# Sample products in groups of four, a partition move by DMA, a last block product ended tile by tile, and eight products on GpSimd, in a streaming encoder step

## The chip, the cores and the metric

The kernel runs on one core of a Trainium2 chip. The core has a matmul engine (PE in the profile, its weight loads PEld), VectorE (DVE), ScalarE (ACT), GpSimd (POOL) and SyncE (SP), which in this kernel issues nearly all transfers. Each engine works off its own list of instructions in order; instructions of different engines meet only at semaphores. Matmuls read from the on-chip memory SBUF and write to PSUM, eight banks of 128 x 512 float32. The metric is the device time of one execution in microseconds (us), the median of several runs.

## The reference, cut to what matters

One layer of a hybrid encoder is applied to 1024 prompt frames and to 32 frames of a running stream (the sample). The change lies in the last product of the layer, the down projection of the feed-forward part, and in the norm and residual behind it:

```
def conv_ffn(xn, buf, w_up, conv_w, conv_b, w_down):
    up = xn @ w_up
    up, buf = causal_dwconv(up, buf, conv_w, conv_b)
    gate, val = jnp.split(up, 2, axis=-1)
    return (jax.nn.gelu(gate, approximate=True) * val) @ w_down, buf
...
    h, ffn_buf = conv_ffn(rms_norm(x, g_ffn_pre[l]), ...)
    x = x + rms_norm(h, g_ffn_post[l])
```

`w_down` is 2816 x 1024, and everything is float32.

## The kernel before, in words

**What runs ahead.** Projections, the three kinds of token mixer, an output projection and the up projection fill the first 1143 us. The up projection leaves the activated rows as 22 tiles `h` of 128 features x (1024 prompt columns and 32 sample columns, with gaps) in DRAM (`h_d`). While it runs, sums of quarters of `w_down` that are needed later are formed in DRAM (`ws_d`).

**Down projection (`down_all`, L1464).** Prompt rows (two halves of 512), features (two halves of 11 tiles, NP = 11) and output columns (two halves of 512) make 2 x 2 blocks on each side, and seven block products P1 to P7 on sums and differences of quarters replace eight. They run in the order P2, P1, P4, P6, P5, P7, P3. `run` (L1480 on) does one of them: for each feature tile p of 0 to 10 it fetches the operands and issues four times three matmuls, one triple for each 128-row tile i, into four PSUM banks. The triple (`mm3`, L100 to L103) is a float32 product from two rounded halves: high by high, high by low, low by high. The halves come from `halves_of` and `split`: ACT casts the high half (L107) and DVE subtracts it from the source (L110). In the profile the line of a matmul is that of `mm3`; the tile names `q` and `x` tell the bank, and `P2w`, `P2h` the operands.

**Raw weights.** `down_raw` (L1419, and L1424 for the summed quarters) loads 512 KB pieces through SP into a ring of two pools with two buffers each. A piece of P1 or P2 holds both column halves, since the sample needs both; the block product uses the left half alone, though `down_operands` splits both. The halves of the activations go through four buffers ("hop"), those of the weights through seven ("op").

**The sample.** Its 32 rows are multiplied with the unsplit weights in float32 while P2 and P1 hold them. `sample_products` (L1461) is called at odd p and at the last p, for both p of the pair and both column halves j: four products, each onto its own 32 partitions of one bank (`s1` in P2, `s2` in P1), so that partitions 0 to 31 hold column half 0 of even p, 32 to 63 half 1 of even p, 64 to 95 half 0 of odd p and 96 to 127 half 1 of odd p. `keep` is the sum of both banks (copy L1545, add L1554). Two float32 matmuls with a selection matrix `sel` (L1558) add the even and odd parts and bring both halves to partitions 0 to 31. The bank of `s2` is one of the three "big" ones that P4 uses next.

**The end.** `norm_of` (L1512 on) squares a 128 x 512 half row tile on ACT with a running sum (L1514) and multiplies it by the gain on DVE (L1515). `close` (L1517 on) turns the sums into a scale by three small operations on POOL (L1518, L220, L221) and, for each column half, multiplies, adds the residual on DVE (L1522) and stores through SP (L1523). The lower four row tiles live in `CA`, the upper four in `CB`. `CB` is complete before P3 begins; upper tiles are normed and closed while P3's first four feature tiles run. `run("P3", ..., 4)` leaves out the last four feature tiles, and the loop behind it issues them row tile by row tile, with the add to `CA` (L1615), the norm and the close of each tile behind it.

**What sets the order.** The program is written in the order above, but each engine's list is laid out by a scheduler that simulates the program and may put a later instruction ahead of an earlier one when its operands are ready sooner. `tc.issue_after(ins)` makes what is issued inside it, on the engine of `ins`, stand behind `ins`. `behind["SP"]` and `behind["POOL"]` are such marks that the kernel keeps already.

Of the kernel before, what the change touches and what calls it, by code (L numbers as in the profile page):

```python
# [8 lines left out]
F32 = mybir.dt.float32  # L9
# [3 lines left out]
AF = mybir.ActivationFunctionType  # L13
ALU = mybir.AluOpType
# [5 lines left out]
DEC = 32  # L20
# [11 lines left out]
GAP_S, SMP, GAP_P = 512, 514, 546  # L32
# [59 lines left out]
def body(ctx: ExitStack, tc: tile.TileContext, a: dict):  # L92
    nc = tc.nc
    act, dve, pool, pe, sp = nc.scalar, nc.vector, nc.gpsimd, nc.tensor, nc.sync
# [5 lines left out]
    def mm3(ps, lh, rh, first, last, **kw):  # L100
        pe.matmul(ps, lh[0], rh[0], start=first, stop=False, **kw)  # L101
        pe.matmul(ps, lh[0], rh[1], start=False, stop=False, **kw)  # L102
        return pe.matmul(ps, lh[1], rh[0], start=False, stop=last, **kw)  # L103

    def split(hi, lo, src, eng=None, heng=None):
        if heng is None:
            act.copy(hi, src)  # L107
        else:
            heng.tensor_copy(hi, src)
        (eng or pool).tensor_tensor(lo, src, hi.bitcast(F32), op=ALU.subtract)  # L110
# [7 lines left out]
    psb = ctx.enter_context(tc.tile_pool(name="psb", bufs=3, space=PSUM))  # L118
# [68 lines left out]
    ident = const("ident", [128, 128])  # L187
# [30 lines left out]
    def rstd_of(out, ss, n, cols, width, eps=EPS):  # L218

        pool.tensor_scalar(out, ss, 1.0 / width, eps, op0=ALU.mult, op1=ALU.add)  # L220
        pool.tensor_tensor(out, out, mhalf[:n, :cols], op=ALU.pow)  # L221
# [996 lines left out]
    behind = {}  # L1218
# [168 lines left out]
    NP = NF // 2  # L1387
# [20 lines left out]
    wraws = {}  # L1408
# [18 lines left out]
    hts = {}  # L1427
# [12 lines left out]
    def halves_of(src, name, pool_, tag, bufs):  # L1440
        t = pool_.tile([128, 2, 512], F32R, tag=tag, name=name, bufs=bufs)
        split(t[:, 0], t[:, 1], src, dve)
        return t[:, 0], t[:, 1]

    def down_operands(ph, kind, p, early=False):
        down_raw(kind, p)
        h = halves_of(ablk(*ASRC[kind], p), f"{kind}h{p}", ph, "hop", 4)
        wp = (ph, "hop", 4) if early else (praw[1], "op", 7)
        if kind in ("P1", "P2"):
            r = wraws[kind, p]  # L1450
            w = [halves_of(r[:, j], f"{kind}w{p}{j}", *wp) for j in range(2)]
        else:
            w = [halves_of(wraws[kind, p // 2][:, p % 2], f"{kind}w{p}", *wp)]
        return h, w

    def sample_products(ps, k, p):

        for q in range(p - p % 2, p + 1):
            for j in range(2):
                r = 64 * (q % 2) + DEC * j  # L1460
                pe.matmul(ps[r:r + DEC], hts[q + NP * k][:, SMP:SMP + DEC], wraws["P2" if k else "P1", q][:, j],  # L1461
                          start=q < 2, stop=q >= NP - 2)

    def down_all(ph, pc, begun, late):  # L1464

        CA = pc.tile([128, 4, 2, 512], F32, name="ca")
        CB = pc.tile([128, 4, 2, 512], F32, name="cb")
        gp = pc.tile([128, 1024], F32, name="gp")
        sp.dma_start(gp, a["grows"][1:2, :].broadcast_to([128, 1024]))
        sel = pc.tile([128, 2 * DEC], F32, name="sel")  # L1470
        dve.tensor_tensor(sel, ident[:, 0:2 * DEC], ident[:, 2 * DEC:], op=ALU.add)
# [5 lines left out]
        def w_banks(name):  # L1477
            return [psf.tile([128, 512], F32, tag="sx", name=f"{name}0", bufs=1)] + \
                [psb.tile([128, 512], F32, tag="big", name=f"{name}{i}", bufs=3) for i in range(1, 4)]

        def run(kind, banks, first, last, each=None, n_end=0):
            end = []
            for p in range(NP):
                ops = begun.pop((kind, p), None) or down_operands(ph, kind, p)
                if p >= NP - n_end:
                    end.append((p, ops))
                    continue
                h, w = ops
                wi = w[0]
                for i in range(4):  # L1490
                    c = slice(128 * i, 128 * i + 128)
                    mm3(banks[i], (h[0][:, c], h[1][:, c]), wi, first and p == 0, last and p == NP - 1, skip_group_check=True)
                if each:
                    each(p, w)
            return end
# [11 lines left out]
        def fourth_sum(p):  # L1507
            f0, f1 = hts[p], hts[p + NP]
            dve.scalar_tensor_tensor(f1[:, :512], f1[:, :512], -1.0, f0[:, :512], op0=ALU.mult, op1=ALU.subtract)

        def norm_of(u, n, src, half, ss):
            c = slice(512 * half, 512 * half + 512)  # L1512
            jk = pc.tile([128, 512], BF16, tag="fjk", name=f"gjk{u}{half}", bufs=2)
            act.activation(jk[:n], src, AF.Square, accum_out=ss[:n, 2 + half:3 + half])  # L1514
            dve.tensor_tensor(src, src, gp[:n, c], op=ALU.mult)  # L1515

        def close(u, n, y, x, ss):  # L1517
            pool.tensor_tensor(ss[:n, 0:1], ss[:n, 2:3], ss[:n, 3:4], op=ALU.add)  # L1518
            rstd_of(ss[:n, 1:2], ss[:n, 0:1], n, 1, 1024)
            for hf in range(2):  # L1520
                c = slice(512 * hf, 512 * hf + 512)
                dve.scalar_tensor_tensor(x[:n, c], y[hf], ss[:n, 1:2], x[:n, c], op0=ALU.mult, op1=ALU.add)  # L1522
# [29 lines left out]
        y8, ss8 = [], scratch(8)  # L1552
        y8t = pc.tile([DEC, 1024], F32, name="y8")
        dve.tensor_tensor(keep, keep, s2, op=ALU.add)  # L1554
        for j in range(2):
            o = psb.tile([128, 512], F32, tag="big", name="so0", bufs=3) if j else \
                psf.tile([128, 512], F32, tag="sx", name="so1", bufs=1)
            pe.matmul(o[:DEC], sel[:, DEC * j:DEC * j + DEC], keep, start=True, stop=True)  # L1558
# [36 lines left out]
        todo = []  # L1595
# [7 lines left out]
        ss_of = {i: scratch(i) for i in range(4)}  # L1603

        def each(p, w):
            if p < 4:
                upper_half(p)
                norm_of(p, 128, CA[:, p, 0], 0, ss_of[p])

        end = run("P3", W, True, True, each, 4)  # L1610
        for i in range(4):
            c = slice(128 * i, 128 * i + 128)
            for p, (h, w) in end:
                mm3(W[i], (h[0][:, c], h[1][:, c]), w[0], False, p == NP - 1, skip_group_check=True)
            dve.tensor_tensor(CA[:, i, 1], CA[:, i, 1], W[i], op=ALU.add)  # L1615
            norm_of(i, 128, CA[:, i, 1], 1, ss_of[i])
            close(i, 128, [CA[:, i, hf] for hf in range(2)], xres[i], ss_of[i])
# [56 lines left out]
    last = [outproj(p2, wo, u) for u in (6, 7)]  # L1674
# [13 lines left out]
    psf = p4s.enter_context(tc.tile_pool(name="psf", bufs=1, space=PSUM))  # L1688
# [206 lines left out]
```

## Time and profile before

The median of three runs is 1406.16 us (1404.16 to 1408.04). The profiled execution took 1408.66 us, of which its span, first to last instruction, is 1406.9 us.

| | |
|---|---|
| PE busy, share of the span | 1355.1 us, 96% |
| DVE busy | 1047.4 us, 74% |
| ACT busy | 718.1 us, 51% |
| POOL busy | 321.2 us, 23% |
| mean granted PE clock | 0.98 |
| P4 to P6 (1238.5 to 1300.0 us), PE busy | 61.5 us |
| P7 (1331 to 1361 us), PE busy | 30.0 us |

Times in a timeline are in us from the start of the span. A row gives start, length, engine, line, operation, output and inputs, shape and how many were merged; in square brackets stands how long the engine had been idle, and what it waited for. Matmuls are pipelined: one shows 0.39 us though the next starts earlier, so distances between starts tell what a matmul costs.

### The profile page before, as it was taken

Reading aid. Unit: us, or ns where it says so; the run is one execution under the profiler, and the core shown is the slowest. Engines: PE = TensorE matmul, PEld = TensorE weight load, DVE = VectorE, ACT = ScalarE, POOL = GpSimd, SP = SyncE. Lnnn points to the kernel's source line nnn. Section 1 sums busy time; section 2 is a strip of 40 time slices with the busy share of each in tenths; the row PEclk is TensorE's granted clock in tenths of the full one; section 3 lists DMA queues with packets and bytes.
Section 4 is the critical chain, followed back from the end, with each engine's and each line's share of the span. In section 5 each row is a group of like instructions: output and inputs, shape, how many; then the busy total and the mean of one; then the engine's idle time right before and its main releaser. Section 6 shows DMA issues by size and latency. Waiting matters only on the chain.

```text
span 1406.9 us, 29277 instructions
## 1 busy us (share of the span) xinstructions
PE 1355.1 (96%) x11476; PEld 1208.4 (86%) x11476; DVE 1047.4 (74%) x1947; ACT 718.1 (51%) x1393; POOL 321.2 (23%) x519
## 2 busy tenths in 40 slices
PE   7999999999999999999899999999999999989996
PEld 6999889898888987777799999999999976568884
DVE  4786468759687669776798888888888875696567
ACT  4556447445474545333764555555455555444451
POOL 5532311235211245213131211121112110000015
PEclk9999999999999989999999999999999999999998
DMA  9599869785899744445315556554554178433353
GB/s 346 190 337 359 273 223 305 227 276 194 275 276 348 235 155 144 142 131 148 124 46 181 144 137 158 144 148 130 160 150 115 62 290 326 162 105 91 97 187 120
DMA packets 126145, 269.52 MB, mean 192 GB/s; under 512 B 23959, under 2 KB 59319, under 8 KB 126007
## 3 DMA queue, kind: packets, MB, share of 16 engines
q1 hardware_dynamic: 113527, 247.46, 52.1%
q0 software_dynamic: 7680, 15.86, 6.0%
q10 hardware_dynamic: 4800, 4.33, 0.9%
q8 instruction: 90, 1.47, 0.4%
q14 instruction: 48, 0.39, 0.1%
HBM read 206.72 MB, written 83.95 MB: 207 GB/s over the span
## 4 chain that ended last, share of the span: by engine, by line
PE 76%; DVE 9%; DMA 7%; ACT 4%; issue 2%; POOL 1%; SPq 0%; POOLq 0%; DVEq 0%; ACTq 0%
PE pux L102 4%; PE pux L101 4%; PE pux L103 4%; PE q L101 3%; PE q L102 3%; PE puw L102 3%; PE pv L101 3%; PE puw L103 3%; PE puw L101 3%; PE pv L103 3%; PE q L103 3%; PE pv L102 3%; PE mi L720 2%; PE zp L101 2%; PE zp L103 2%; PE zp L102 2%
## 5 line engine op out<-in xcount | busy, mean ns | idle before, releaser
L1341 DVE SCALAR_TENSOR_TENSOR y<-uu,fconv_sb,y 128x1060 f32<-128x1060 f32 x88 | 116.3, 1321 | 35.8 <-ACT y L1339 35.3
L1277 ACT COPY c<-pux 128x272 f32<-128x272 f32 (+1 forms) x132 | 49.2, 375 | 53.8 <-PE pux L103 50.1
L1339 ACT ACTIVATE y<-uu,fconv_sb 128x1060 f32<-128x1060 f32 x44 | 56.2, 1276 | 13.6 <-POOL uu L1335 11.9
L101 PE MATMUL zp<-woh,ch 128*128 128x512 f32 (+1 forms) x144 | 60.1, 419 | 1.9 <-DVE z L1156 1.2
L101 PE MATMUL pv<-wt_0h,xh 128*128 128x256 f32 (+2 forms) x195 | 57.4, 295 | 4.0 <-ACT xh L321 4.0
L102 PE MATMUL zp<-wol,ch 128*128 128x512 f32 (+1 forms) x144 | 59.0, 410 | 0.0
L1338 POOL COPY fhalo<-uu 128x2 f32<-128x2 f32 x44 | 17.5, 397 | 181.5 <-DVE uu L1282 181.5
L103 PE MATMUL zp<-woh,cl 128*128 128x512 f32 (+1 forms) x144 | 58.8, 409 | 0.0
L1518 POOL TENSOR_TENSOR gss<-gss 128x1 f32<-128x1 f32 (+1 forms) x9 | 7.8, 871 | 220.5 <-ACT gjk L1514 134.1
L103 PE MATMUL pv<-wt_0h,xl 128*128 128x256 f32 (+2 forms) x195 | 56.5, 290 | 0.4 <-DVE xl L322 0.4
L103 PE MATMUL pv<-wt_1h,xl 128*128 128x256 f32 (+2 forms) x195 | 56.6, 290 | 0.0
L102 PE MATMUL pv<-wt_0l,xh 128*128 128x256 f32 (+2 forms) x195 | 56.1, 288 | 0.1
L102 PE MATMUL pv<-wt_1l,xh 128*128 128x256 f32 (+2 forms) x195 | 56.2, 288 | 0.0
L101 PE MATMUL pv<-wt_1h,xh 128*128 128x256 f32 (+2 forms) x195 | 56.1, 288 | 0.0
L220 POOL TENSOR_SCALAR hrs<-hss 128x5 f32<-128x5 f32 (+3 forms) x27 | 9.8, 364 | 163.1 <-DVE hss L922 161.7
L431 POOL TENSOR_TENSOR vg<-vth,gh 128x256 f32<-128x256 f32 (+1 forms) x36 | 30.6, 850 | 63.8 <-DMA vm<-v_d 22.4
L1335 POOL COPY uu<-uu 128x2 f32<-128x2 f32 x44 | 34.4, 781 | 45.0 <-DVE uu L1282 44.1
L101 PEld LDWEIGHTS pv<-wt_0h,xh 128*128 128x128 f32 (+1 forms) x195 | 36.9, 189 | 5.6 <-ACT xh L321 4.9
L851 DVE TENSOR_TENSOR Qz<-x,qe 128x128 f32<-128x128 f32 (+1 forms) x106 | 29.9, 300 | 12.8 <-PE sc L720 12.0
L815 DVE COPY_PREDICATED P<-masks_sb,sc 128x352 f32<-128x352 int32 (+1 forms) x44 | 29.8, 676 | 12.4 <-PE sc L720 12.2
L103 PEld LDWEIGHTS pv<-wt_0h,xl 128*128 128x128 f32 (+1 forms) x195 | 36.9, 189 | 1.2 <-DVE xl L322 0.9
L103 PEld LDWEIGHTS pv<-wt_1h,xl 128*128 128x128 f32 (+1 forms) x195 | 36.9, 189 | 0.6 <-issue 0.2
(1716 smaller groups left out, 5465.8 us busy)
## 6 DMA issues: line engine op xcount, KB each, us to landing
wrP<-in_w_dn SPq DMA_DIRECT2D x27, 512.0 KB, 5.3
h_d<-y SPq DMA_DIRECT2D x22, 530.0 KB, 3.1
ht<-h_d SPq DMA_DIRECT2D x22, 530.0 KB, 6.8
wt_0r<-in_w_tok SPq DMA_DIRECT2D x21, 512.0 KB, 4.9
wt_1r<-in_w_tok SPq DMA_DIRECT2D x21, 512.0 KB, 6.6
ws_d<-in_w_dn POOLq DMA_DIRECT2D x20, 512.0 KB, 8.9
wrP<-ws_d SPq DMA_DIRECT2D x20, 512.0 KB, 3.6
wt_0l<-lt_d SPq DMA_DIRECT2D x14, 512.0 KB, 3.8
```

The costliest lines, as they stand in the source:

```text
L101: pe.matmul(ps, lh[0], rh[0], start=first, stop=False, **kw)
L102: pe.matmul(ps, lh[0], rh[1], start=False, stop=False, **kw)
L103: return pe.matmul(ps, lh[1], rh[0], start=False, stop=last, **kw)
L431: pool.tensor_tensor(o[:n], th[:n], gh[:n, c0:c0 + 256], op=ALU.mult)
L720: fn(*args, **kw)
L815: dve.copy_predicated(dst, mk.broadcast_to([n, 11, *mk.shape[2:]]), src)
L851: dve.tensor_tensor(Qp[:, 2 * i, :, :n // 2].rearrange("p e (m c) -> p e m c", c=c), second(x4[:, f:f + 1], c).broadcast_to([128, 2, n // ...
L1277: kept[name] = act.copy(t, ps)
L1335: pool.tensor_copy(u[:, GAP_P:GAP_P + 2], u[:, GAP_S - 2:GAP_S])
L1338: behind["POOL"] = pool.tensor_copy(fhalo[:, j, :], u[:, NCOL - 2:NCOL])
L1339: act.activation(y, u, AF.Identity, scale=fconv[:, j, 2:3], bias=fconv[:, j, 3:4])
L1341: dve.scalar_tensor_tensor(y, uu[i][:, s:s + NCOL], fconv[:, j, s:s + 1], y, op0=ALU.mult, op1=ALU.add)
```

## The change

- `down_operands` splits only the left half of a P1 or P2 piece.
- `run` keeps the last matmul of each triple in `behind["PE"]`, and `sample_products` issues its four products behind it.
- `sel` and its two matmuls are gone. Three DMAs on SP move partitions 32 to 127 of `keep`, in quarters of 32, to partitions 0 to 31 of a tile `quarter`. The sums of the quarters are two DVE operations, called after feature tile 9 of P5, followed there by the sample's norm and close, which stood behind P4.
- The gain product and square of the left half of the four lower row tiles move from P3 (feature tiles 0 to 3) to P5 (1, 3, 5, 7).
- The gain products of the upper row tiles, eight of 128 x 512, go from DVE to POOL.
- In the loop at the end, each row tile's twelve matmuls stand behind the last matmul of the row tile before.

```diff
@@ down_operands
-            w = [halves_of(r[:, j], f"{kind}w{p}{j}", *wp) for j in range(2)]
+            w = halves_of(r[:, 0], f"{kind}w{p}", *wp)
...
@@ sample_products
-        for q in range(p - p % 2, p + 1):
-            for j in range(2):
-                r = 64 * (q % 2) + DEC * j
-                pe.matmul(ps[r:r + DEC], hts[q + NP * k][:, SMP:SMP + DEC], wraws["P2" if k else "P1", q][:, j],
-                          start=q < 2, stop=q >= NP - 2)
+        with tc.issue_after(behind["PE"].ins):
+            for q in range(p - p % 2, p + 1):
+                for j in range(2):
+                    r = 64 * (q % 2) + DEC * j
+                    pe.matmul(ps[r:r + DEC], hts[q + NP * k][:, SMP:SMP + DEC], wraws["P2" if k else "P1", q][:, j],
+                              start=q < 2, stop=q >= NP - 2)
...
@@ run
-                    mm3(banks[i], (h[0][:, c], h[1][:, c]), wi, first and p == 0, last and p == NP - 1, skip_group_check=True)
+                    behind["PE"] = mm3(banks[i], (h[0][:, c], h[1][:, c]), w, first and p == 0, last and p == NP - 1,
+                                       skip_group_check=True)
...
@@ norm_of
-        def norm_of(u, n, src, half, ss):
+        def norm_of(u, n, src, half, ss, eng=dve):
...
-            dve.tensor_tensor(src, src, gp[:n, c], op=ALU.mult)
+            eng.tensor_tensor(src, src, gp[:n, c], op=ALU.mult)
...
@@ behind P1
-        for j in range(2):
-            o = psb.tile([128, 512], F32, tag="big", name="so0", bufs=3) if j else \
-                psf.tile([128, 512], F32, tag="sx", name="so1", bufs=1)
-            pe.matmul(o[:DEC], sel[:, DEC * j:DEC * j + DEC], keep, start=True, stop=True)
-            c = slice(512 * j, 512 * j + 512)
-            act.activation(y8t[:, c], o[:DEC], AF.Copy, scale=1.0 - 2.0 * j)
-            y8.append(y8t[:, c])
+        quarter = pc.tile([DEC, 3, 512], F32, name="quarter")
+        for b in range(3):
+            sp.dma_start(quarter[:, b], keep[DEC * (b + 1):DEC * (b + 2)])
...
@@ behind P4
-        for j in range(2):
-            norm_of(8, DEC, y8[j], j, ss8)
-        close(8, DEC, y8, xs8, ss8)
...
@@ P5
-        run("P5", W, True, True, lambda p, w: fourth_sum(p))
+        ss_of = {i: scratch(i) for i in range(4)}
+
+        def after_p6(p, w):
+            fourth_sum(p)
+            if p in (1, 3, 5, 7):
+                norm_of(p // 2, 128, CA[:, p // 2, 0], 0, ss_of[p // 2])
+            if p == 9:
+                y8, ss8 = [keep[:DEC], quarter[:, 0]], scratch(8)
+                dve.tensor_tensor(y8[0], y8[0], quarter[:, 1], op=ALU.add)
+                dve.scalar_tensor_tensor(y8[1], y8[1], -1.0, quarter[:, 2], op0=ALU.mult, op1=ALU.subtract)
+                for j in range(2):
+                    norm_of(8, DEC, y8[j], j, ss8)
+                close(8, DEC, y8, xs8, ss8)
+
+        run("P5", W, True, True, after_p6)
...
@@ upper_half, each, and the loop at the end
-                norm_of(u, 128, CB[:, i, hf], hf, ss)
+                norm_of(u, 128, CB[:, i, hf], hf, ss, pool)
...
-                norm_of(p, 128, CA[:, p, 0], 0, ss_of[p])
...
-            for p, (h, w) in end:
-                mm3(W[i], (h[0][:, c], h[1][:, c]), w[0], False, p == NP - 1, skip_group_check=True)
+            with tc.issue_after(behind["PE"].ins):
+                for p, (h, w) in end:
+                    behind["PE"] = mm3(W[i], (h[0][:, c], h[1][:, c]), w, False, p == NP - 1, skip_group_check=True)
```

More of the change, by code (lines that the diff above doesn't have):

```diff
@@ L1450, in down_operands @@
             r = wraws[kind, p]
-            w = [halves_of(r[:, j], f"{kind}w{p}{j}", *wp) for j in range(2)]
+            w = halves_of(r[:, 0], f"{kind}w{p}", *wp)
         else:
-            w = [halves_of(wraws[kind, p // 2][:, p % 2], f"{kind}w{p}", *wp)]
+            w = halves_of(wraws[kind, p // 2][:, p % 2], f"{kind}w{p}", *wp)
         return h, w
     def sample_products(ps, k, p):
-        for q in range(p - p % 2, p + 1):
-            for j in range(2):
-                r = 64 * (q % 2) + DEC * j
-                pe.matmul(ps[r:r + DEC], hts[q + NP * k][:, SMP:SMP + DEC], wraws["P2" if k else "P1", q][:, j],
-                          start=q < 2, stop=q >= NP - 2)
+        with tc.issue_after(behind["PE"].ins):
[4 more added lines that the diff above has]
+                              start=q < 2, stop=q >= NP - 2)
     def down_all(ph, pc, begun, late):
@@ L1469, in down_all @@
         sp.dma_start(gp, a["grows"][1:2, :].broadcast_to([128, 1024]))
-        sel = pc.tile([128, 2 * DEC], F32, name="sel")
-        dve.tensor_tensor(sel, ident[:, 0:2 * DEC], ident[:, 2 * DEC:], op=ALU.add)
         act.activation(gp[:, 512:], gp[:, 512:], AF.Copy, scale=-1.0)
@@ L1488, in run @@
                 h, w = ops
-                wi = w[0]
                 for i in range(4):
                     c = slice(128 * i, 128 * i + 128)
-                    mm3(banks[i], (h[0][:, c], h[1][:, c]), wi, first and p == 0, last and p == NP - 1, skip_group_check=True)
+                    behind["PE"] = mm3(banks[i], (h[0][:, c], h[1][:, c]), w, first and p == 0, last and p == NP - 1,
+                                       skip_group_check=True)
                 if each:
@@ L1551, in down_all @@
         run("P1", X, True, False, rows_of(0, s2))
-        y8, ss8 = [], scratch(8)
-        y8t = pc.tile([DEC, 1024], F32, name="y8")
         dve.tensor_tensor(keep, keep, s2, op=ALU.add)
-        for j in range(2):
-            o = psb.tile([128, 512], F32, tag="big", name="so0", bufs=3) if j else \
-                psf.tile([128, 512], F32, tag="sx", name="so1", bufs=1)
-            pe.matmul(o[:DEC], sel[:, DEC * j:DEC * j + DEC], keep, start=True, stop=True)
-            c = slice(512 * j, 512 * j + 512)
-            act.activation(y8t[:, c], o[:DEC], AF.Copy, scale=1.0 - 2.0 * j)
-            y8.append(y8t[:, c])
+        quarter = pc.tile([DEC, 3, 512], F32, name="quarter")
+        for b in range(3):
+            sp.dma_start(quarter[:, b], keep[DEC * (b + 1):DEC * (b + 2)])
         for i in range(4):
@@ L1594, in down_all @@
             dve.tensor_tensor(CB[:, i, 1], X[i], CB[:, i, 1], op=ALU.subtract)
-        todo = []
         def upper_half(i):
@@ L1599, in upper_half @@
             for hf in range(2):
-                norm_of(u, 128, CB[:, i, hf], hf, ss)
+                norm_of(u, 128, CB[:, i, hf], hf, ss, pool)
             close(u, 128, [CB[:, i, hf] for hf in range(2)], xres[u], ss)
-        ss_of = {i: scratch(i) for i in range(4)}
         def each(p, w):
```

## The prediction

> **What bounds the kernel now.** I read three views: the busy table over stretches of the last 263 us (the down projection; columns: stretch, length, busy time of PE, PEld, DVE, ACT, POOL, granted clock, DMA share, GB/s), the list of what PE waited for there, and the timeline around each edit.
>
> ```profile
> span 1406.9 us, 29277 instructions
> ```
>
> ```profile
> 1143.80:1190.30 46.50, 46.50 (x196) 28.36 (x196) 30.31 (x47) 25.25 (x45) 2.03 (x3) 1.00 0.94 359
> 1190.30:1230.90 40.60, 40.00 (x171) 24.10 (x169) 25.80 (x42) 19.50 (x37) 0.00 (x0) 1.00 0.54 182
> 1230.90:1238.50 7.60, 3.64 (x7) 0.59 (x5) 7.60 (x14) 4.62 (x9) 0.00 (x0) 0.66 0.40 127
> ...
> 1300.00:1331.00 31.00, 31.00 (x135) 24.90 (x134) 14.43 (x24) 14.80 (x27) 0.00 (x0) 1.00 0.33 94
> ...
> 1361.00:1393.50 32.50, 32.45 (x140) 25.73 (x138) 26.74 (x45) 14.70 (x38) 17.20 (x12) 1.00 0.32 124
> 1393.50:1406.90 13.40, 0.00 (x0) 0.00 (x0) 9.57 (x15) 2.60 (x8) 6.42 (x12) 0.63 0.42 157
> ```
>
> ```profile
> PE so L1558 <- DVE keep L1554: 4.0, 1, 4.0
> PE x L101 <- ACT P1w L107: 0.6, 1, 0.6
> ```
>
> PE is busy in all of P2, P1, P5 and P3 and in the whole projection waited for others 4.6 us. So a matmul taken off PE's queue comes off the end, unless its operands then come late. Two stretches are not PE's: 7.6 us between P1 and P4 (3.64 busy, clock 0.66), and 13.4 us behind the last matmul.
>
> **Term A, sample products in fours.** They issue 88 instructions, two for each of 44 products.
>
> ```profile
> L1461 PE MATMUL s<-wrP,ht x88: 592/605/617, 1143.8 to 1230.4; 128*32 128x512 f32 x88
> ```
>
> ```profile
> 1154.76 0.40 PE L103 MATMUL q<-P2w,P2h 128*128 128x512 f32 x1
> 1155.08 1.05 PE L1461 MATMUL s<-wrP,ht 128*32 128x512 f32 x4
> 1156.07 0.50 PE L101 MATMUL q<-P2w,P2h 128*128 128x512 f32 x1
> 1156.40 0.39 PE L102 MATMUL q<-P2w,P2h 128*128 128x512 f32 x1
> ...
> 1225.92 1.07 PE L1461 MATMUL s<-wrP,ht 128*32 128x512 f32 x8
> 1226.92 0.50 PE L101 MATMUL x<-P1w,P1h 128*128 128x512 f32 x1
> ```
>
> Eight instructions (four products on four 32-column strips) hold PE from 1225.92 to 1226.92, 1.00 us; four hold it 0.99. A group's price does not depend on its size. Projection matmuls start 0.233 us apart (the row of four at 1392.36, quoted at the end: (1.09 - 0.39) / 3), a block of twelve takes 2.80; from 1154.76 to 1156.40 lie 1.64 us where two steps would be 0.47, so a group costs 1.17 us. The rows of this line form 20 groups: three of eight, fifteen of four, two of two (24 + 60 + 4 = 88). Issued at odd p and at p = 10, all ready at once behind their block, they form six in P2 and six in P1. Eight groups fewer are 8 x 1.17 = 9.4 us.
>
> What takes some of it back is the ring of four raw weight buffers. A buffer is free when its products are done; the first of a pair now waits for the end of the second's block. SP already waits for that:
>
> ```profile
> SPq L1419 <- PE s L1461: 31.3, 12, 5.9
> ```
>
> Landings of these loads, in 1160 to 1180 us and in 1200 to 1215 us (last number):
>
> ```profile
> wrP<-in_w_dn SPq DMA_DIRECT2D x5, 512.0 KB, 11.1
> ```
>
> ```profile
> wrP<-in_w_dn SPq DMA_DIRECT2D x4, 512.0 KB, 3.3
> ```
>
> A pair lasts 2 x 2.80 + 1.17 = 6.77 us. The buffer freed at its start must be loaded, then cast and split (0.6 + 0.7 us, ACT's and DVE's rows of 128x512 at the end below) before the next pair: landings up to about 5.4 us cost nothing. P1's 3.3 fits, P2 with its DMA share of 0.94 does not always. The middle of the two rows, 7.2 us, would cost 1.8 at each of P2's four refills and leave 2.2 of 9.4. Nearer to the free end, since only a part of P2 is full, I take 2.3 us in all, a little over one such landing: A = 7.1, bounds 2.2 and 9.4. Dropping the unused right-half splits takes 22 casts from ACT and 22 subtracts from DVE; PE's matmuls cover both engines there (25.25 and 30.31 busy of 46.50), so I count nothing; without that cover it could only gain.
>
> **Term B, the quarters by DMA.**
>
> ```profile
> 1229.92 1.05 PE L1461 MATMUL s<-wrP,ht 128*32 128x512 f32 x4
> 1234.93 3.59 PE L1558 MATMUL so<-keep,sel 128*32 128x512 f32 x4 [3.96 <-DVE keep L1554]
> 1238.45 0.80 PE L101 MATMUL q<-P4w,P4h 128*128 128x512 f32 x1
> ...
> 1240.46 0.40 PE L103 MATMUL q<-P4w,P4h 128*128 128x512 f32 x1
> ```
>
> The last group holds PE until 1229.92 + 0.98 = 1230.90. The selection matmuls stand ahead of P4 in PE's queue and wait for the add to `keep`. The sixth P4 matmul starts at 1240.46, as if P4 had begun at 1240.46 - 5 x 0.233 = 1239.29. Removing the four matmuls closes up to 1239.29 - 1230.90 = 8.4 us. P4's blocks 0 and 1 are split by then. What is late next: the fourth bank of P4 is freed by the same add to `keep`, now 9 x 0.233 = 2.1 us after the start, with DVE busy all 7.6 us of that stretch; and the weights of block 2, whose buffer is freed one group before P1's end (3.97 us). I take 1.4 us for both, B = 7.0; bounds 8.4 and 3.7 (the add as late as now, 3.96, plus one split).
> The three quarter DMAs queue on SP behind the same add; P4's later weights are behind them if they come first, which is inside that bound. Nobody reads the quarters before P5's last blocks, 60 us on. The sample's two sums, norms and closing products, and four 128-row products, go to P5, where DVE has 14.43 of 31.00 us busy: twelve operations at 0.6 fit; a closing product that waits for POOL there holds up the splits behind it, which are a block ahead. Zero, bounds 0 and -2.
>
> **Term C, the end.** First DVE alone, then ACT and PE, then POOL.
>
> ```profile
> 1386.33 0.70 DVE L110 TENSOR_TENSOR P3h<-ht,P3h 128x512 fp32r<-128x512 f32 x1
> 1392.79 2.48 DVE L1615 TENSOR_TENSOR ca<-ca,q 128x512 f32<-128x512 f32 x4 [5.76 <-PE q L103]
> ...
> 1401.44 2.08 DVE L1522 SCALAR_TENSOR_TENSOR fr<-ca,gss,fr 128x512 f32<-128x512 f32 x3 [0.44 <-POOL gss L221]
> ```
>
> ```profile
> 1392.36 1.09 PE L103 MATMUL q<-P3w,P3h 128*128 128x512 f32 x4
> ...
> 1393.52 0.63 ACT L1514 ACTIVATE gjk<-ca 128x512 bf16<-128x512 f32 x1 [10.60 <-DVE ca L1615]
> ```
>
> ```profile
> 1378.43 3.58 POOL L220 TENSOR_SCALAR gss<-gss 128x1 f32<-128x1 f32 x1
> ...
> 1394.60 0.19 POOL L220 TENSOR_SCALAR gss<-gss 128x1 f32<-128x1 f32 x1
> 1394.87 0.55 POOL L221 TENSOR_TENSOR gss<-gss,mhalf 128x1 f32<-128x1 f32 x1
> ```
>
> Now all four tiles end together: the last four matmuls go up to 1393.45, and four adds, squares, scale chains and eight products follow one another until 1403.52; the span ends 3.4 later, 13.45 us behind PE. With tiles in turn, 12 x 0.233 = 2.8 us apart, tile 3 alone is left: the add 0.73 (1392.79 to ACT's start), the square and POOL's chain 1.90 (1393.52 to 1394.87 + 0.55), two products 1.4 (three take 2.08), a hand-over 0.1, the last store 3.4: 7.5 us. Gain 5.9.
> Against it: tile 0 needs all of blocks 7 to 10 at its start. The last split now runs at 1386.33 to 1387.03. PE would start tile 0 at 1393.45 - 11.2 = 1382.25 and want block 10 for its last third, at 1384.3: 2.7 us late if DVE is as late as now. DVE loses twelve products of 0.6 here (four to P5, eight to POOL), 7.2 us, but now waits in line for POOL: each upper-half closing product needs POOL's two products and three small operations (about 1.1 us, 0.19 and 0.55 being two of them).
>
> ```profile
> L926 POOL TENSOR_TENSOR cat<-cat,gt 128x384 f32<-128x384 f32 x8 | 8.9, 1109 | 3.7 <-DVE cat L924 3.7
> ```
>
> No POOL product of 512 columns is in the trace; by the row above, 1.109 x 512/384 = 1.5 us, eight are 12 us. The same tiny operation took 0.19 us with DVE idle and 3.58 while DVE ran split after split, so the two engines shut each other out. Bounds: no stall; or all of it in series before the last split: DVE 26.74 - 7.2 - 0.7 (the first add behind the last matmul) = 18.8, POOL 12 + 4 x 1.1 = 16.4, together 35.2 in the 23.3 us from 1361.0 to 1384.3: 11.9 late. I take 2 us, near the free end, since PE waited for nothing while DVE was at 26.74 of 32.50. C = 5.9 - 2.0 = 3.9, bounds -6.0 and 5.9.
> The Trainium skill speaks against this edit: SBUF — State Buffer, section "SBUF: two separate sides", says that VectorE operations with two SBUF inputs and GpSimd hold one port pair by exclusive lock, each for its whole instruction. The rows show one half of it, POOL shut out; DVE's splits stayed at 0.70. By the rule DVE would also stand for POOL's whole 12 us, and C would come out at its low end.
>
> **Sum.** 7.1 + 7.0 + 3.9 = 18.0 us. The profiled execution took 1408.66 us with its span of 1406.9; 18.0 less is 1390.7. The runs' median is 1406.16, 2.5 below it, so the forecast is **1388.2 us**.
>
> **Rivals.**
> *Weights starve (slower).* If freed buffers refill as slowly as in P2's worst rows, 11.1 us, each pair stalls 11.1 - 5.4 = 5.7 us; P2's four refilled groups cost 23, two more at P1's start 11: 34 against 18 + 2.3 already counted, 1406.2 - 20.3 + 34 = 1420. It decides from about 3.4 us a group, landings of 8.8. For: DMA share 0.94, SP's 31.3 us of waiting. Against: SP held back puts fewer loads in flight, and P1 lands in 3.3. Chance 0.05.
> *POOL becomes the bound of the end.* All 11.9 us come: 18.0 - 9.9 = 8.1, 1398. For: the 3.58 row and the skill's rule. Against: the eight sums that open this stretch read PSUM for one operand, and the split of block 10 can run before a closing product. Chance 0.22.
> *The groups don't form.* If the program's scheduler still parts the products (the order is only "behind the block"), A is nothing: 18.0 - 7.1 = 10.9, 1395. Against: all four become ready together. Chance 0.08.
> The forecast, within about 5 us, has 0.56; 0.09 is left for schedules with other stalls.
>
> **Numbers.** Bounds: A + B + C at best 9.4 + 8.4 + 5.9 = 23.7, 1382; at worst 2.2 + 3.7 - 2 - 6.0 = -2.1, 1408. The range 1381 to 1401 leaves out the starved case and the worst sums. I call 0.3%, 4.2 us, what a measurement can tell. Faster: forecast, POOL, parted groups and some of the rest, 0.89; same 0.05; slower 0.06.
>
> **What would show it.** A: twelve groups of the sample line, eight instructions each but for the two last, P2 and P1 shorter by 7; wrong if PE waits for weight splits after each group. B: P4's first matmul within 0.5 us of the last group, no idle over 2 us. C: about 2.8 us between the four final adds, the span ending some 8 us behind the last matmul; wrong if PE idles before tile 0's last matmuls with DVE waiting for POOL.

## The result, and the profile after

The changed kernel takes 1396.60 us (median of four runs, 1394.32 to 1397.74) against 1406.38 for the kernel before: ratio 0.9933, 95% interval 0.9917 to 0.9949. That is 9.8 us less, where 18.0 were forecast; the time lies in the stated range. The span of the profiled execution, which took 1394.32 us, fell by 14.4 us:

```profile
span 1392.5 us, 29239 instructions
```

3.5 of these 14.4 come ahead of the down projection and are not the change's. Up to the down projection PE has the same matmuls in the same order in both, yet the projection's first matmul starts at 1143.84 us before and at 1140.38 after; in the runs of this study it starts anywhere from 1138.5 to 1143.8. As a rule it goes with the clock granted ahead of it: PE had half its clock for 41.0 us before and for 27.3 after, for 20.5 in the two profiles that start earliest and for 41.0 in the three that start latest. So times of single runs scatter by some 5 us, and the lengths of stages below say more than the medians do. I cut the down projection at four points: its first matmul (of P2 or of the sample), P4's first matmul, PE's end, and the span's end (the tail). In us:

| | first to P4 | P4 to PE's end | tail | together |
|---|---|---|---|---|
| before | 94.6 | 155.0 | 13.4 | 263.1 |
| after | 84.6 | 158.2 | 9.4 | 252.1 |

The first column fell by 10.0, of which 7.55 is the closed hole between P1 and P4 (1230.90 to 1238.45) and 2.5 all that is left of the sample groups. The second rose by 3.2 though the slow start of P4 (0.84) is gone from it, so PE lost 4.0 elsewhere. The third fell by 4.1.

In the changed kernel the sample's matmuls have line 1462, the gain products 1514, the closing products 1521, the final adds 1616. First PE's timeline in P2, at the end of block 4 and the start of block 5 (blocks are the feature tiles p, counted from 0):

```profile
1160.20 0.39 PE L102 MATMUL q<-P2w,P2h 128*128 128x512 f32 x1
1160.44 0.40 PE L103 MATMUL q<-P2w,P2h 128*128 128x512 f32 x1
1163.31 1.60 PE L101 MATMUL q<-P2w,P2h 128*128 128x512 f32 x4 [2.47 <-ACT P2w L107]
1164.71 0.63 PE L102 MATMUL q<-P2w,P2h 128*128 128x512 f32 x1
```

PE has 60 of P2's matmuls behind it there, five blocks, and waits 2.47 us for the cast of block 5's weights (the expectations further down call it block 4). Then eight steps take 0.43 us instead of 0.23, 1.6 us more: the granted clock is 0.50 from 1163.90 to 1167.31. PE waited 4.8 us in P2 altogether, where it had waited for nothing. What the stretches before it show (columns as in the prediction; the last two are DMA share and GB/s):

```profile
1145.00:1150.00 5.00, 3.96 (x16) 2.94 (x17) 3.46 (x7) 3.60 (x6) 0.37 (x2) 1.00 0.74 289
1150.00:1155.00 5.00, 5.00 (x26) 3.17 (x25) 5.00 (x7) 2.55 (x5) 0.00 (x0) 1.00 0.10 30
1155.00:1160.00 5.00, 5.00 (x26) 3.11 (x25) 2.23 (x3) 0.74 (x2) 0.00 (x0) 1.00 1.00 316
```

From 1150 to 1155 the DMA engines do next to nothing, 30 GB/s, in the stage that needs them most; the kernel before, which entered P2 3.5 us later, moved 411 there:

```profile
1150.00:1155.00 5.00, 5.00 (x26) 3.30 (x18) 4.07 (x9) 3.16 (x5) 1.45 (x2) 1.00 1.03 411
```

The waits of SP from 1136 to 1156 tell why:

```profile
SPq L1756 <- POOL uu L1335: 6.6, 1, 6.6
SPq L1419 <- PE s L1462: 4.6, 1, 4.6
```

SP first stands at the store of the halo (the convolution's last columns, an output of the layer), which waits for POOL, then at the load of block 4's weights, whose buffer is held until the first pair's products are done at 1153.1; every h load queues behind. That load goes out 12.8 us after the projection's first matmul, where the kernel before issued it after 2.9. Then all of them come at once and the loads crawl. Block 4's weights land after 3.3 us, at 1156.49, still in time. Those of block 5, whose load was issued at 1155.05, take some 7.5 and are cast only here:

```profile
1162.63 0.62 ACT L107 CAST P2w<-wrP 128x512 fp32r<-128x512 f32 x1 [0.58 <-DMA wrP<-in_w_dn]
```

The hole is in the loading, the bill comes at block 5.

At P1's end there is nothing left of the wait:

```profile
1224.01 1.05 PE L1462 MATMUL s<-wrP,ht 128*32 128x512 f32 x4
1224.99 0.50 PE L101 MATMUL q<-P4w,P4h 128*128 128x512 f32 x1
```

In P3 the groups of DVE's splits from 1346 to 1372 us (count, busy time, mean ns) and DVE's timeline at the end of this stretch:

```profile
L110 DVE TENSOR_TENSOR P3h<-ht,P3h 128x512 fp32r<-128x512 f32 x9 | 10.1, 1140 | 0.0
L110 DVE TENSOR_TENSOR P3w<-wrP,P3w 128x512 fp32r<-128x512 f32 x6 | 6.3, 1047 | 0.0
```

```profile
1360.85 1.78 DVE L110 TENSOR_TENSOR P3w<-wrP,P3w 128x512 fp32r<-128x512 f32 x1
1362.55 1.78 DVE L110 TENSOR_TENSOR P3h<-ht,P3h 128x512 fp32r<-128x512 f32 x1
...
1367.91 2.74 DVE L1521 SCALAR_TENSOR_TENSOR fr<-cb,gss,fr 128x512 f32<-128x512 f32 x4
1370.56 1.89 DVE L110 TENSOR_TENSOR P3h<-ht,P3h 128x512 fp32r<-128x512 f32 x3
```

A split takes 0.69 us alone and up to 1.78 beside POOL's products. POOL's timeline has two products beside the two splits of 1360.85 and 1362.55:

```profile
1360.39 3.38 POOL L1514 TENSOR_TENSOR cb<-cb,gp 128x512 f32<-128x512 f32 x2
```

The last three splits come behind four closing products, and PE waits for them inside tile 0, after which its clock is at half for 3.41 us (0.50 in the last row here, where 1.00 is the rule):

```profile
1368.84 0.40 PE L102 MATMUL q<-P3w,P3h 128*128 128x512 f32 x1
1371.30 0.50 PE L103 MATMUL q<-P3w,P3h 128*128 128x512 f32 x1 [2.07 <-DVE P3h L110]
```

```profile
1372.11:1375.52 3.41, 3.41 (x10) 2.63 (x9) 1.06 (x3) 0.72 (x2) 0.00 (x0) 0.50 0.05 17
```

2.07 us of waiting and some 1.6 of slow matmuls (eight steps of 0.43) make 3.7 of the 4.0 lost.

### The profile page after: what moved, and what is told of

The parts are those of the page before. It is cut to its first block, busy times and chain, and to the rows that moved or that the text cites. A ratio compares the mean times of both kernels' runs of the same rounds, so it can differ in the third digit from the quotient of the medians.

```text
span 1392.5 us, 29239 instructions
## 1 busy us (share of the span) xinstructions
PE 1339.2 (96%) x11472; PEld 1202.9 (86%) x11472; DVE 1038.2 (75%) x1918; ACT 707.5 (51%) x1369; POOL 322.3 (23%) x527
## 4 chain that ended last, share of the span: by engine, by line
PE 70%; DVE 11%; DMA 8%; ACT 5%; issue 2%; POOL 2%; SPq 1%; DVEq 0%; POOLq 0%; ACTq 0%
PE pux L101 4%; PE pux L102 4%; PE pux L103 4%; PE puw L102 3%; PE puw L103 3%; PE puw L101 3%; PE pv L101 3%; PE pv L103 3%; PE pv L102 3%; PE q L103 2%; PE q L101 2%; PE q L102 2%; PE x L101 2%; PE x L102 2%; PE x L103 2%
## 5 line engine op out<-in xcount | busy, mean ns | idle before, releaser
L1339 ACT ACTIVATE y<-uu,fconv_sb 128x1060 f32<-128x1060 f32 x44 | 56.2, 1278 | 12.8 <-POOL uu L1335 11.4
L1517 POOL TENSOR_TENSOR gss<-gss 128x1 f32<-128x1 f32 (+1 forms) x9 | 14.2, 1574 | 103.7 <-ACT gjk L1513 103.7
L851 DVE TENSOR_TENSOR Qz<-x,qe 128x128 f32<-128x128 f32 (+1 forms) x106 | 29.9, 299 | 10.7 <-PE sc L720 10.2
L102 PEld LDWEIGHTS pv<-wt_0l,xh 128*128 128x128 f32 (+1 forms) x195 | 36.9, 189 | 0.6 <-POOL wt_0l L110 0.5
L1335 POOL COPY uu<-uu 128x2 f32<-128x2 f32 x44 | 26.9, 612 | 44.6 <-DVE uu L1282 43.7
```

The costliest lines, as they stand in the source:

```text
L851: dve.tensor_tensor(Qp[:, 2 * i, :, :n // 2].rearrange("p e (m c) -> p e m c", c=c), second(x4[:, f:f + 1], c).broadcast_to([128, 2, n // ...
L1335: pool.tensor_copy(u[:, GAP_P:GAP_P + 2], u[:, GAP_S - 2:GAP_S])
L1339: act.activation(y, u, AF.Identity, scale=fconv[:, j, 2:3], bias=fconv[:, j, 3:4])
```

## The experiments

All medians are against the kernel before, timed alongside (1405.4 to 1406.6). Stages are as above; where a sample group stands ahead of P2, the first column is 0.97 us longer than the same from P2's first matmul, which the expectations use.

| | first to P4 | P4 to PE's end | tail | median | ratio (95%) |
|---|---|---|---|---|---|
| products free | 86.5 | 157.2 | 9.7 | 1398.25 | 0.9936 (0.9911 to 0.9961) |
| five buffers | 81.8 | 156.6 | 9.6 | 1392.22 | 0.9895 (0.9872 to 0.9918) |
| norms on DVE | 87.6 | 154.6 | 9.6 | 1391.79 | 0.9902 (0.9873 to 0.9931) |
| end free | 85.5 | 154.5 | 10.7 | 1393.14 | 0.9906 (0.9880 to 0.9931) |
| quarters alone | 87.1 | 154.3 | 13.3 | 1398.32 | 0.9952 (0.9933 to 0.9971) |
| buffers and norms | 83.2 | 154.6 | 9.6 | 1391.20 | 0.9907 (0.9890 to 0.9924) |
| first pair singly | 87.8 | 158.1 | 9.4 | 1395.62 | 0.9933 (0.9911 to 0.9955) |
| late close | 83.3 | 154.6 | 8.0 | 1391.29 | 0.9906 (0.9891 to 0.9921) |
| norms, end free | 84.1 | 154.3 | 12.7 | 1396.14 | 0.9931 (0.9912 to 0.9949) |
| first pair free | 84.2 | 156.6 | 9.6 | 1392.98 | 0.9909 (0.9885 to 0.9932) |
| all repairs | 82.2 | 154.6 | 8.0 | 1390.20 | 0.9880 (0.9862 to 0.9899) |
| repairs, four buffers | 84.5 | 154.8 | 8.0 | 1390.53 | 0.9879 (0.9863 to 0.9895) |

**Products free.** In the changed kernel:

```diff
-        with tc.issue_after(behind["PE"].ins):
-            for q in range(p - p % 2, p + 1):
+        for q in range(p - p % 2, p + 1):
```

> The changed kernel, with the sample products no longer tied behind their block; they then stand in 18 groups instead of 12. From the first P2 matmul to the first P4 matmul the changed kernel takes 84.6 us (1140.38 to 1224.99). Theory: fours save 1.17 us a group, but nearly all of it is given back because a raw buffer is held for a pair; free products load earlier, PE's 4.8 us of idle time in P2 shrink to under 1.5, and the stretch is 84.6 + 6 x 1.17 - 4.8 to 6.7 = 85 to 87, the time 1397 to 1399. Rival: the idle time comes from something else (the right half no longer split, late h tiles) and stays; then the stretch is 84.6 + 7.0 = 91.6 and the time 1403 or more.

The scheduler parts the products again, 18 groups, and PE waits nowhere in P2, though the right halves are still not split there, so the waits are the tie's. The stretch is 85.5 from P2's first matmul, inside 85 to 87, the time 1398.25. The tie's saving and its waits nearly cancel.

**Five buffers.**

```diff
-        turn[0] ^= 1
-        r = (ph[0] if turn[0] else praw[0]).tile(..., bufs=2)
+        turn[0] = (turn[0] + 1) % 5
+        odd = turn[0] % 2
+        r = (praw[0] if odd else ph[0]).tile(..., bufs=2 if odd else 3)
```

> The changed kernel with a third raw buffer in one of the two pools, so five instead of four. Theory: SP, stuck on a held buffer, keeps the h loads behind it and leaves the DMA engines idle near the start of P2, and the backlog makes PE wait 2.47 us at block 4; with a fifth buffer the wait at block 4 and its slow matmuls go, the stretch of 84.6 falls by 4 to 6 us to 79 to 81, and the time is 1391 to 1393. Rival: the bytes of P2 are the limit whatever the buffers; then the stretch stays within 1 us of 84.6 and the time at 1396 to 1397.

The stretch fell by 2.8 to 81.8, short of the 4 to 6 expected, the time to 1392.22. The empty window is full:

```profile
1150.00:1155.00 5.00, 2.28 (x13) 0.89 (x6) 4.64 (x6) 4.41 (x8) 0.00 (x0) 1.00 1.00 371
```

PE's wait of 2.47 us at block 5 is gone, but it waits 2.03 us earlier, at block 2 in this very window, and 1.23 near 1178, where DMA runs at 415 GB/s. So the hold was a cause; full DMA engines beside a waiting PE point to the bytes of P2 as a second, which no run tests alone.

Nor does this run test the buffer alone. The scheduler put the first pair right behind block 1, 24 matmuls of P2 ahead of it instead of 33, so its products ran 7.2 us after P2's first matmul instead of 11.7. And no stretch of low clock fell into P2 here. Like with like, four buffers against five, with twelve groups each: 84.1 (norms, end free) against 81.8 without a low stretch in P2, 84.6 and 85.5 (end free) against 83.2 and 83.3 (two runs below) with one. Five buffers with the earlier pair are worth 1.3 to 2.3.

**Norms on DVE.**

```diff
-                norm_of(u, 128, CB[:, i, hf], hf, ss, pool)
+                norm_of(u, 128, CB[:, i, hf], hf, ss)
```

> The changed kernel with the eight gain products of the upper row tiles back on DVE. Theory: POOL's products hold the port that DVE's splits need; six splits take 1.78 instead of 0.69 us, and the last split comes late. Without them all splits take 0.69, PE's wait of 2.07 us before tile 0 ends and the slow matmuls after it go, 3 to 4 us in all: 1392.5 to 1393.6. Rival: DVE is the limit of this stretch either way, and its eight products more (4.8 us) stand ahead of the last splits; then PE still waits 1.5 to 3 us there and the time is 1396 to 1398.

PE no longer waits in P3; from P4 to PE's end 154.6 instead of 158.2. P3 begins 6.0 us later in this profile (1354.31 against 1348.30), so the 26 us that match those above are 1352 to 1378. The splits in them:

```profile
L110 DVE TENSOR_TENSOR P3h<-ht,P3h 128x512 fp32r<-128x512 f32 x9 | 6.0, 681 | 0.0
L110 DVE TENSOR_TENSOR P3w<-wrP,P3w 128x512 fp32r<-128x512 f32 x6 | 4.1, 681 | 0.0
```

From 1.05 to 1.14 us down to 0.68: the same fifteen splits take 10.1 us instead of 16.4. DVE, with eight products more (5.2 us), was no busier in this stretch (24.71 us, not 25.16). The rival falls. In the changed kernel DVE stood idle for POOL's scales only 0.4 us in this stretch, so the longer splits weigh far more than that wait.

**End free.**

```diff
-            with tc.issue_after(behind["PE"].ins):
-                for p, (h, w) in end:
-                    behind["PE"] = mm3(...)
+            for p, (h, w) in end:
+                mm3(...)
```

> The changed kernel with the last matmuls no longer tied tile behind tile. Theory: tile order itself is worth 3 to 4 us between PE's end and the span's end (9.4 us instead of 13.4), and costs most of that again in the wait for the last split, so without it PE's wait goes and the tail grows: the time stays within 1.5 us, 1395 to 1398. Rival: the tail is set by POOL's and DVE's order and not by the matmuls' order, then the tail stays at 9 to 10 us and the time falls to 1392 to 1393; or the wait stays and the time rises to 1400.

PE's wait went, as the theory said, but the tail grew only to 10.7: P4 to the span's end is 165.2 instead of 167.5, and the time fell to 1393.14, below what I expected. Without the stretch of low clock in the changed kernel's P3 (1.6 us) the two would be nearly equal. DVE's final adds show that the scheduler had spaced the tiles itself; three are done before PE's end at 1378.74, and the last starts 2.9 us after it, behind gain and closing products:

```profile
1373.88 1.28 DVE L1615 TENSOR_TENSOR ca<-ca,q 128x512 f32<-128x512 f32 x2 [2.18 <-PE q L103]
1375.35 0.69 DVE L1514 TENSOR_TENSOR ca<-ca,gp 128x512 f32<-128x512 f32 x1 [0.20 <-ACT gjk L1513]
1375.98 0.69 DVE L1615 TENSOR_TENSOR ca<-ca,q 128x512 f32<-128x512 f32 x1
...
1381.63 0.68 DVE L1615 TENSOR_TENSOR ca<-ca,q 128x512 f32<-128x512 f32 x1
```

**Norms, end free.** The two edits above together.

> The changed kernel with the upper gain products on DVE and the last matmuls not tied: against the run with the products on DVE alone (154.6 us from P4's first matmul to PE's end, tail 9.6) this shows what the tile order is worth when nothing makes PE wait. Theory: the scheduler ends the tiles nearly together, so the tail grows to 11 to 13 us, PE's part stays at 154.5, and the sum of both rises by 1.5 to 3.5 us over 164.2. Rival: the scheduler's own order spaces the last tiles enough, the tail stays below 10.5 and the tie is worth nothing.

Here the tiles end close together, and the tail is 12.7 against 9.6 with the tie and the same stretch ahead of it (154.3 and 154.6). Tile order is worth 2.7 us once nothing stalls, as the theory had it, and nothing where POOL's products make tile 0 wait (167.5 with the tie, 165.2 without).

**Quarters alone.** In the kernel before:

```diff
-        for j in range(2):
-            o = ...
-            pe.matmul(o[:DEC], sel[:, DEC * j:DEC * j + DEC], keep, start=True, stop=True)
-            ...
+        quarter = pc.tile([DEC, 3, 512], F32, name="quarter")
+        for b in range(3):
+            sp.dma_start(quarter[:, b], keep[DEC * (b + 1):DEC * (b + 2)])
```

The two sums of quarters stand ahead of the sample's norm behind P4.

> The kernel before, with nothing changed but the sample's partition move: three quarter DMAs in place of the selection matmuls; sums, norm and close stay behind P4. Theory: the four matmuls and the wait ahead of P4 cost 8.4 us, and P4 has its operands; the last sample group (ending 0.98 after its start) and P4's first matmul lie within 0.2 us of each other, and the time falls by 7.5 to 8.5 to 1398. Rival: P4's splits and sums on DVE (29.33 of 31.80 us busy there) were made during the wait, and without it PE waits inside P4; then PE idles 3 us or more between P4's start and P6 and the time is 1401 or more.

From the first matmul to PE's end 241.3 instead of 249.6: 8.3 us, and PE waits nowhere behind P1. The median fell by 7.1 (ratio 0.9952), a little less than the 7.5 to 8.5 expected. The rival falls.

**Buffers and norms.** Five buffers and the norms on DVE.

> The changed kernel with both repairs, five raw buffers and the upper gain products on DVE. Theory: the two losses are separate, so they add: the stretch from P2's first to P4's first matmul is 80 to 83 us as with the fifth buffer alone (81.8), the stretch from P4's first matmul to PE's end 154.5 as with the products on DVE alone (154.6), the time 1387 to 1389. Rival: the losses have one cause (the schedule as a whole), and one repair takes in most of the other; then 1391 to 1392.

The second stage is as the norms alone had it (154.6). The first is 83.2 and not 81.8: the same wait of 2.03 us was followed by low clock here and not there. The median, 1391.20, is 2 us above what I expected, in the rival's range and no better than each alone (1392.22 and 1391.79); the scatter ahead of the projection blurs it, and against the rival speak the stages alone.

**First pair singly.**

```diff
-            for q in range(p - p % 2, p + 1):
+            for q in range(p if p < 2 and k else p - p % 2, p + 1):
...
-                if p % 2 or p == NP - 1:
+                if p % 2 or p == NP - 1 or (k and p == 0):
```

> The changed kernel, four raw buffers, but in P2 the products of p = 0 and of p = 1 are issued each behind its own block: thirteen groups. Theory: the hold of the first buffer at the start of P2 is what empties the DMA queue (share 0.10 from 1150 to 1155 us), so freeing it one block earlier ends the wait at block 4 (2.5 us and 1.9 of slow matmuls) for one group more (1.17 us): the stretch is 80 to 83 instead of 84.6 to 87.6, the time 1393 to 1394. Rival: SP is stuck there on something else (the store of the halo, which waits for POOL's copies); then the wait at block 4 stays and the time is 1397.

Missed: 87.8, and the waits stay, as in the rival. Block 0's products ran at 1150.50, 12.0 us after P2's first matmul; the pair in the changed kernel ran after 11.7. They are tied to block 0's last triple, the one of the fourth bank, and in PE's list that triple stands behind three banks of blocks 0 to 2: 30 matmuls of P2 are ahead of the products, where a block has 12. The tie is to a late matmul, so finer pairing frees nothing. The rival's wait at the halo's store (6.6 us, as in the changed kernel) is there too, but SP then stands 5.4 us more for these products. That the bank is late because the up projection still used it was only argued.

**First pair free.**

```diff
-        with tc.issue_after(behind["PE"].ins):
+        with ExitStack() if k and p < 2 else tc.issue_after(behind["PE"].ins):
```

> The changed kernel with only the first pair of P2 not tied; its products then stand ahead of and inside block 0, fourteen groups in all. In the changed kernel they wait for the last triple of block 1, and that waits for the fourth bank, which the up projection holds. Theory: tying to a matmul of the late bank is what holds the first two raw buffers, stops SP and empties the DMA queue; freed, the DMA share from 1150 to 1155 us is over 0.9 instead of 0.10, the 2.5 us wait at block 4 goes, and the stretch from P2's first to P4's first matmul, 84.6 to 87.8 with four buffers so far, falls to 80 to 83; time 1392 to 1394. Rival: later pairs stall just as much once the first doesn't; the stretch stays at 84 or more and the time at 1396.

Half a miss: 84.2 (83.2 from P2's first matmul), with two groups more (2.3 us), time 1392.98. SP does not wait at the halo's store here, and the waits up to 1160 are gone, but PE waits 2.02 and 2.48 us in later blocks. The hole in the loading only moves:

```profile
1150.00:1155.00 5.00, 5.00 (x23) 4.00 (x22) 4.15 (x7) 2.70 (x5) 0.00 (x0) 1.00 0.62 247
1155.00:1160.00 5.00, 5.00 (x26) 3.15 (x25) 3.28 (x5) 1.14 (x2) 0.00 (x0) 1.00 0.32 67
```

SP now stands 8.9 us at the second pair, so the hold of a buffer makes a hole without the halo's store, and with four buffers the second pair's hold counts as well as the first's.

**Late close.** Five buffers, norms on DVE, and:

```diff
-            dve.tensor_tensor(CA[:, i, 1], CA[:, i, 1], W[i], op=ALU.add)
+            add = dve.tensor_tensor(CA[:, i, 1], CA[:, i, 1], W[i], op=ALU.add)
             norm_of(i, 128, CA[:, i, 1], 1, ss_of[i])
-            close(i, ...)
+            if i:
+                with tc.issue_after(add.ins):
+                    close(i - 1, ...)
+        close(3, ...)
```

> Five raw buffers, gain products on DVE, and at the end the closing products of tile i stand behind the add of tile i + 1 on DVE. Theory: the last add now waits 1.5 to 1.8 us behind closing products that wait for POOL; put ahead of them it starts with PE's end, and the tail falls from 9.4 to 9.6 us to 7.5 to 8.2, the time 1385 to 1387. Rival: the tail is the last tile's own chain and store, then it stays above 9 and the time equals that of the same kernel without this order.

In the changed kernel the last add stood behind tile 2's closing product, which stood waiting for POOL, though PE had ended at 1383.14:

```profile
1384.03 0.75 DVE L1521 SCALAR_TENSOR_TENSOR fr<-ca,gss,fr 128x512 f32<-128x512 f32 x1 [0.44 <-POOL gss L221]
1384.70 0.68 DVE L1616 TENSOR_TENSOR ca<-ca,q 128x512 f32<-128x512 f32 x1
```

With the order turned round it starts with PE's end (1381.49):

```profile
1381.53 0.69 DVE L1617 TENSOR_TENSOR ca<-ca,q 128x512 f32<-128x512 f32 x1 [0.18 <-PE q L103]
1382.14 1.41 DVE L1522 SCALAR_TENSOR_TENSOR fr<-ca,gss,fr 128x512 f32<-128x512 f32 x2
```

The tail is 8.0 in all three runs with this order. 1.6 us of 1390 do not show in the medians (1391.29 against 1391.20), so the gain is read from the profile alone; the expected time of 1385 to 1387 was missed.

**All repairs**, with five buffers and with four: late close, norms on DVE, first pair free.

> Five buffers, first pair free, gain products on DVE, closing products behind the next add. Theory: the repairs add, stretch 79 to 81.5, 154.6 from P4's first matmul to PE's end, tail 8.0: 1386 to 1389. Rival: the bytes of P2 set a floor near the 81.8 to 83.3 that five buffers gave, and the first pair makes no difference on top; 1390 to 1391.

> The same with four raw buffers: if the first pair is the whole cause of the starved stretch, it is within 1 us of the kernel with five buffers; if the hold of every pair counts, it is 2 to 4 us slower.

Both were measured: 1390.20 and 1390.53. The stages are 82.2 and 84.5. A sample group more (fourteen against thirteen, 1.17 us) and a stretch of low clock (some 1.3 us) in the run with four explain these 2.3 us, so here the fifth buffer shows no gain of its own, and none in the medians. Whether the hold of every pair costs time stays open. Both beat the changed kernel (0.9880 and 0.9879 against 0.9933, the intervals do not touch), by about 6 us. The medians lie at the rival's end of what I expected: the first pair adds little on top of five buffers (82.2 against 81.8 to 83.3), though from P2's first matmul it is 81.2, in the range of 79 to 81.5.

## Why the prediction was right, and where its sizes were off

The direction and the three places were right; the forecast gain was nearly twice the measured one. The time alone, 1396.6, would fit the rivals of parted groups (1395) and of POOL as the bound (1398) better than the forecast; the stages decide against both.

- **A, forecast 7.1, came out at 2.5** in the profile pair. Over the four profiles with four buffers, twelve groups and the same P2 (84.6, 87.6, 85.5, 84.1; mean 85.5 against 87.1) it is 1.6, below my lower bound of 2.2. What mainly tells these four apart is the low clock: none of it in P2 at 84.1, one stretch at 84.6 and 85.5, two at 87.6. The groups formed as forecast, twelve of them at the price of 1.17 us: 9.4 was there. The failed step is the allowance of 2.3 us, "a little over one such landing": in the changed kernel the waits took 4.8 and the slow matmuls 1.6. I priced a landing that is long; what happened is that SP stopped at the held buffer and the DMA engines stood idle, which no landing time of the kernel before shows. A sign of it was there: the DMA share of the kernel before falls to 0.32 from 1160.0 to 1162.5, without a wait of PE. My view of the first pair was wrong too: I let its products follow block 1, but they follow the triple of the late fourth bank. The rival of starving weights named the wait that came, put it down to slow refills and not to a stopped queue, and priced it far too high, at 34 us. That the hold of the buffers makes the waits is shown by the run with free products and the one with the first pair free, and supported by those with five buffers.
- **B, forecast 7.0, came out at 8.4**, its free end (the changed kernel's 0.98 us from the last group to P4 is the group itself). The run with the quarters alone gives 8.3. Neither the late add to `keep` nor block 2's weights made PE wait.
- **C, forecast 3.9, came out at 0.1.** The tail gained 4.1 of the 5.9: the last add waited 1.5 us behind a closing product that waited for POOL, a DVE wait that I had left out. And PE lost 4.0 and not 2.0: the wait itself was 2.07, as forecast, which is partly luck, since I chose 2 between bounds of 0 and 11.9 and did not count it out. Some 1.6 us of slow matmuls came on top, which I had not priced; two runs with the same wait escaped them (156.6 from P4 to PE's end instead of 158.2). That POOL's products are the cause is shown by the run that puts them back, 3.6 us shorter. I had weighed the lock too lightly: in the rows before, DVE's splits stayed at 0.70 beside POOL's tiny operations, but beside a product of 512 columns they took 1.78. That is the other half of what the Trainium skill states (SBUF — State Buffer, "SBUF: two separate sides"), and here the trace agrees. The low end that I drew from it did not come: the fifteen splits took 6.3 us longer, not POOL's whole 12.
- **Costed at nothing**: the dropped splits and the moved norms. PE waits nowhere in P5 and P7, so no loss came from the norms. What the dropped splits alone are worth was not tried.
- **No rival came whole.** POOL as the bound of the end came to a third of its price: 4.0 us of a possible 11.9.

It stays open how the time of P2 divides between SP's stops and the sheer bytes: five buffers leave 81.8 to 83.3, where 87.1 - 9.4 = 77.7 would be ideal, and no run took bytes away.

## What to carry to other kernels

When instructions are put together to save time on one engine, ask what each of them holds until it has run: here the later products kept a load buffer, and the queue behind that load fed the whole stage. Tie an instruction to the one that it must follow, not to the last of a loop, which may wait for something else. Before handing work to a second engine, ask what it shares with the first, and whether the first then waits for its result in its own queue: here eight products handed over made the splits 6.3 us longer and cost PE 3.6.

## What the runs showed of the hardware that was not expected

Waits of 1.9 to 2.5 us already lower PE's clock at times, and the traces show when. PE's wait of 2.47 us that ended at 1163 and its wait of 2.07 that ended at 1371 (changed kernel) were each followed by 3.41 us at a granted clock of 0.50, with steps of 0.43 us; after 2.02 us at 1169 in the run with the first pair free the steps took 0.23 at once. In every profile the clock changes only on a grid of 3.41 us, which lies differently in each. Of the twenty waits of 1.97 to 2.49 us in P2 and P3, nine were followed by half the clock: there PE was idle for 1.90 to 2.47 us within one step of the grid. In the other eleven the border of a step parted the wait, and no step had more than 1.90. (Two low stretches more, at P2's start, followed two shorter waits close together, with 1.5 and 1.7 us idle in the step.) So the same wait of 2.07 to 2.09 us in P3 makes 156.6, 156.6 and 157.2 us from P4's first matmul to PE's end where the clock held, and 158.1 and 158.2 where it fell. The Trainium skill (TensorE: Matmul & The Clock Gate, "What's actually happening") tells of a clock halved after an idle window of about 3.4 us that runs freely. The half clock and the free window agree with these traces, but here 1.9 us of idle time in a window were enough.

GpSimd's product of 128 x 512 took 1.30 us with DVE on PSUM operands and up to 1.75 beside DVE's splits; scaled from 384 columns I had 1.5.
